# Keys and queries of layer two turned in 32 by 32 blocks by VectorE and moved between partition blocks by ScalarE, in place of transposes on TensorE

## The chip, the cores and the metric

The kernel runs on one core of a Trainium2 chip. The metric is the device time of one execution in microseconds (us). Engines are named as the profile names them: PE is TensorE (PEld its weight loads), DVE is VectorE, ACT is ScalarE, POOL is GpSimd, SP is the engine that issues most DMAs. SBUF is the memory that the engines work on, 128 partitions wide; PSUM is where PE writes its products.

## The reference, cut to what matters

The reference is two layers over 256 tokens of width 2048. The first is a gated linear attention and isn't touched. The second is softmax attention with 16 heads of 128. Keys and queries are projected, normed for each token and head, and multiplied:

```python
proj = h @ w_in.astype(h.dtype)
q = rms_norm(proj[..., :B_INNER].reshape(bsz, t, B_HEADS, B_HEAD_DIM), q_norm_w)
k = rms_norm(proj[..., B_INNER:2 * B_INNER].reshape(bsz, t, B_HEADS, B_HEAD_DIM), k_norm_w)
...
s = jnp.einsum('bchd,bmhd->bhcm', q_n, k_n).astype(jnp.float32) * scale + bias
...
p = jax.nn.softmax(s, axis=-1).astype(v_n.dtype)
return jnp.einsum('bhcm,bmhd->bchd', p, v_n)
```

The norm runs over the head's 128 values of one token, so it is done with tokens on the partitions. The scores contract over these 128 values, so PE needs them on the partitions. Between the two, each head's block of 128 tokens by 128 values has to be transposed.

## The kernel before

All large products are made in chunks. A chunk is 256 rows of a weight matrix by 512 columns: one load of 512 KB from SP's queue into `wt`, one cast on ACT into a rounded part `whi` (line 211), one subtraction on DVE into the remainder `wlo` (line 212), then twelve matmuls on PE in the kind `tokens` (lines 282 to 287, issued at line 259). For each of two row blocks and two token halves these are: activations times `whi`, activations times `wlo`, the activations' own remainder times `whi`. `wt` has four buffers, `whi` and `wlo` have three, so the cast of a chunk can start only when PE has finished the chunk three before it, and the load of a chunk only when the remainder four before it is done. Eight chunks make a block of 512 columns, which is four heads.

`plan` (lines 141 to 166) fixes the order of the chunks: for each of four groups of heads a block of keys, then one of queries, then four blocks of values, then the output projection. Everything else is background work: generators in the lists `bgq` and `bg2`, each cut into steps by `yield`. `block(kind, xb, rate)` calls `tick` after each piece of a chunk, and `tick` runs `rate` steps for each 128 rows, so a block gives 16 steps at rate 1. A scheduler then puts the instructions of each engine into one fixed order, which the engine follows, waiting where an operand isn't there.

For each block of keys or queries the background runs `qk_norm` (lines 1030 to 1063), during the block that follows. ACT squares the block out of PSUM (line 1035), DVE sums by head (1038), POOL makes the reciprocal roots (1040, 1042), DVE multiplies (1047) into a tile `n` with tokens on the partitions. Then PE transposes the eight 128 by 128 pieces against a unit matrix (1057), four into each of two PSUM tiles, and ACT copies each into its place in `dl`: for keys with a scale that holds both norm weights (1062), for queries without (1060). `attend` (1065) follows the queries of a group: score products on PE (1076, 1077), bias and maximum on DVE (1085, 1087), exponentials on ACT (1089), the division on DVE (1095, 1097), the transposition of the weights on PE (1103) and their copy on ACT (1104).

Of the kernel before, what the change touches and what calls it, by code (L numbers as in the profile page):

```python
# [10 lines left out]
AF = mybir.ActivationFunctionType  # L11
# [3 lines left out]
P = 128  # L15
D = 2048
T = 256
# [20 lines left out]
def tile_hybrid_trunk(  # L38
# [12 lines left out]
    act, dve, pool, pe = nc.scalar, nc.vector, nc.gpsimd, nc.tensor  # L51
# [9 lines left out]
    def ps_small():  # L61
        return pss.tile([P, 512], F32, name="pss", tag="pss")

    def wk(tag, bufs=None):

        return work.tile([P, 4, T], F32, name=tag, tag=tag, bufs=bufs)
# [24 lines left out]
    ident = const.tile([P, P], F32, name="ident")  # L91
# [162 lines left out]
    def drain():  # L254
        while now or bgq or bg2:
            step()
# [34 lines left out]
    def chunk(kind, ps, xb, rate=1, pre=None):  # L291
        i = state["use"]
        state["use"] += 1
        while state["next"] < min(i + 1 + LOOK, len(plan)):
            fetch()
        hi, lo = fetched.pop(i)
        kc = KC * 512 // plan[i][3]
        ks = [plan[i][2] * kc + j for j in range(kc)]
        f, ns = KINDS[kind]
        if kind == "half":  # L300
            ps = ps if isinstance(ps, list) else [ps[:, s] for s in range(2)]
            if pre is not None:
                pre(ks[-1])
            for _ in features2(ps, hi, lo, ks, xb):
                tick(rate / 2)
            return
        for j, kt in enumerate(ks):
            if pre is not None:
                pre(kt)
            for s in range(ns):  # L310
                f(ps[:, s], s, j, kt, hi, lo, xb)
                tick(rate / ns)

    def acc(kind):

        shape = {"features": [P, 4, T], "half": [P, 2, 2, T], "tokens": [P, 2, 512]}[kind]
        return psp.tile(shape, F32, name="psp", tag="psp")

    def block(kind, xb, rate=1, pre=None):
        ps = acc(kind)  # L320
        for _ in range(CPH if kind == "half" else CPB):
            chunk(kind, ps, xb, rate, pre)
        return ps
# [33 lines left out]
    def split_tiles():  # L357
        return slot("xb", 32, F32R).rearrange("p (k a t) -> p k a t", k=KT, a=2)
# [34 lines left out]
    xb = split_tiles()  # L393
# [622 lines left out]
    xb = hmem["x"]  # L1016
# [13 lines left out]
    def qk_norm(ps, scale, dst):  # L1030

        ssn = tiny.tile([P, 2, 4], F32, name="ssn", tag="so")
        rn = tiny.tile([P, 2, 4], F32, name="rn", tag="ro")
        sq = wk("cv").rearrange("p h t -> p (h t)")
        act.activation(out=sq, in_=ps.rearrange("p t d -> p (t d)"), func=AF.Square)
        yield 1
        yield 1
        dve.reduce_sum(out=ssn, in_=sq.rearrange("p (t h d) -> p t h d", t=2, d=P), axis=AX.X)  # L1038
        for t in range(2):
            pool.tensor_scalar(out=ssn[:, t, :], in0=ssn[:, t, :], scalar1=1.0 / P, scalar2=bmem["uh"][:, t:t + 1],  # L1040
                               op0=ALU.mult, op1=ALU.add)
        pool.tensor_tensor(out=rn, in0=ssn, in1=nhalf[:, :8].rearrange("p (t h) -> p t h", t=2), op=ALU.pow)  # L1042
        yield 1
        yield 1
        n = wk("cv").rearrange("p h t -> p (h t)").rearrange("p (t d) -> p t d", t=2)
        for t in range(2):
            dve.tensor_tensor(out=n[:, t, :].rearrange("p (h d) -> p h d", d=P),  # L1047
                              in0=ps[:, t, :].rearrange("p (h d) -> p h d", d=P),
                              in1=rn[:, t, :].unsqueeze(2).broadcast_to([P, 4, P]), op=ALU.mult)
        yield 1  # L1050
        yield 1
        for p in range(2):
            pt = ps_small()
            for i in range(2):
                c = (2 * p + i) * P
                for t in range(2):
                    pe.transpose(pt[:, i * T + t * P:i * T + (t + 1) * P], n[:, t, c:c + P], ident)  # L1057
            d = dst[:, 2 * p:2 * p + 2, :].rearrange("p h t -> p (h t)")
            if scale is None:
                act.copy(out=d, in_=pt)  # L1060
            else:
                act.activation(out=d, in_=pt, func=AF.Copy, scale=scale)
            yield 1

    def attend(gi, qn, kn):
# [75 lines left out]

    for gi in range(4):
        c = 1024 * (gi % 2)
        psk = block("tokens", xb)
        if gi == 0:
            drain()
        kn, qn = (hmem["m"][:, b + c:b + c + 1024].rearrange("p (h t) -> p h t", h=4) for b in (8192, 10240))
        bgq.append(qk_norm(psk, bmem["wqk"][:, 0:1], kn))
        psq = block("tokens", xb)
        bgq.append(qk_norm(psq, None, qn))  # L1150
        bgq.append(attend(gi, qn, kn))

# [101 lines left out]
```

## Time and profile before

| What | Value |
|---|---|
| Median of three runs | 1005.47 us (1005.43 to 1006.92) |
| The profiled execution, timed as a whole | 1006.75 us |
| Its span, first to last instruction | 1004.0 us |
| Mean granted clock of PE | 0.999 |
| First and last transposes of keys and queries on PE (line 1057) | 648 and 820 us into the span |
| Idle time of PE over the span, sum of its waits | 2.4 us |

A page of the profile gives for each engine its busy time, its share of the span and its instructions. The chain that ended last is followed back from the last instruction; PE holds 97% of it. In rows of time the columns are start, length, engine, line, operation, what it writes and reads, shapes and count, and in brackets how long the engine stood idle before it and what ended that. In rows of groups they are busy time, mean length of one in ns, idle time before.

### The profile page before, as it was taken

The page shows a single profiled execution, that of the slowest core. Times are in us where ns is not written, and L with a number is a line of the kernel's source. Part 1 is how long each engine was busy: PE and PEld are TensorE (multiplying, and loading weights), DVE is VectorE, ACT ScalarE, POOL GpSimd, SP SyncE. Part 2 cuts the span into 40 slices and gives each one's busy share as a digit, 9 for nine tenths or more (in the row PEclk, how much of TensorE's full clock was granted, in tenths as well). Part 3 has the DMA queues.
Part 4 walks back from the last instruction along what each step waited for, and adds up shares of the span by engine and source line. Part 5 has one row for each costly group of instructions (what it writes and reads, how often), then busy time and mean ns, then how long its engine had stood idle before and what let it go on. Part 6 is the DMA issues. An engine that isn't in the chain of part 4 may idle for free.

```text
span 1004.0 us, 15429 instructions
## 1 busy us (share of the span) xinstructions
PE 997.8 (99%) x5959; PEld 869.5 (87%) x5959; DVE 692.1 (69%) x1129; ACT 528.0 (53%) x791; POOL 61.7 (6%) x78
## 2 busy tenths in 40 slices
PE   9999999999999999999999999999999999999998
PEld 8988888888888899899988888888888888888887
DVE  7789879997998777665767555556565656555554
ACT  8457865564456554544654444446464645444432
POOL 1000001131000000001000000110101010000000
PEclk9999999999999999999999999999999999999999
DMA  9565665555755554545765766665555565555662
GB/s 292 186 185 152 170 187 149 157 157 153 208 166 167 148 148 137 167 137 183 231 193 173 232 207 211 192 184 168 170 166 179 156 188 147 168 169 173 216 216 88
DMA packets 138345, 177.55 MB, mean 177 GB/s; under 512 B 7968, under 2 KB 98464, under 8 KB 138272
## 3 DMA queue, kind: packets, MB, share of 16 engines
q1 hardware_dynamic: 136832, 172.12, 57.8%
q0 software_dynamic: 1152, 4.19, 1.2%
q8 instruction: 46, 0.75, 0.3%
q10 hardware_dynamic: 288, 0.26, 0.1%
q14 instruction: 27, 0.22, 0.1%
HBM read 174.46 MB, written 2.10 MB: 176 GB/s over the span
## 4 chain that ended last, share of the span: by engine, by line
PE 97%; ACT 1%; DMA 1%; DVE 0%; issue 0%; SPq 0%
PE psp L259 86%; PE pss L601 2%; PE pss L259 1%; PE pss L1057 1%; PE pss L1077 1%; PE pss L1133 1%; PE pss L833 1%; DMA g<-in_xT_dram 1%; PE pss L501 1%; PE pss L1103 1%; ACT whi L211 0%; PE pss L856 0%; PE pss L857 0%; PE pss L840 0%; PE pss L858 0%
## 5 line engine op out<-in xcount | busy, mean ns | idle before, releaser
L212 DVE TENSOR_TENSOR wlo<-wt,whi 128x1024 fp32r<-128x1024 f32 (+2 forms) x324 | 391.5, 1212 | 255.5 <-ACT whi L211 251.4
L211 ACT CAST whi<-wt 128x1024 fp32r<-128x1024 f32 (+2 forms) x324 | 336.5, 1039 | 392.3 <-PE psp L259 346.4
L259 PE MATMUL psp<-whi,xb 128*128 128x512 f32 x1024 | 319.5, 392 | 0.0
L259 PE MATMUL psp<-xb,whi 128*128 128x512 f32 (+1 forms) x1088 | 259.4, 380 | 0.3 <-DVE ev L330 0.2
L259 PEld LDWEIGHTS psp<-whi,xb 128*128 128x128 f32 x1024 | 192.0, 188 | 38.9
L259 PEld LDWEIGHTS psp<-xb,whi 128*128 128x128 f32 x1088 | 195.5, 189 | 34.4 <-DVE ev L330 0.6
L259 PE MATMUL psp<-wlo,xb 128*128 128x512 f32 x512 | 200.5, 392 | 0.0
L259 PE MATMUL psp<-xb,wlo 128*128 128x256 f32 x1024 | 148.0, 284 | 0.5 <-DVE wlo L212 0.4
L259 PEld LDWEIGHTS psp<-xb,wlo 128*128 128x128 f32 x1024 | 137.0, 191 | 6.3 <-DVE wlo L212 1.1
L259 PE MATMUL psp<-g,whi 128*128 128x512 f32 (+1 forms) x608 | 132.9, 347 | 0.3 <-DVE ev L330 0.2
L259 PEld LDWEIGHTS psp<-g,whi 128*128 128x128 f32 x608 | 104.7, 190 | 13.3 <-DVE ev L330 0.6
L259 PEld LDWEIGHTS psp<-wlo,xb 128*128 128x128 f32 x512 | 96.2, 188 | 19.6
L259 PE MATMUL psp<-g,wlo 128*128 128x256 f32 x480 | 82.4, 284 | 0.3 <-DVE wlo L212 0.3
L259 PEld LDWEIGHTS psp<-g,wlo 128*128 128x128 f32 x480 | 69.8, 191 | 2.3 <-DVE wlo L212 0.5
L529 DVE SCALAR_TENSOR_TENSOR cv<-raw,sm,cv 128x255 f32<-128x255 f32 (+2 forms) x144 | 63.9, 478 | 3.4 <-ACT cv L527 3.2
L527 ACT ACTIVATE cv<-raw,sm 128x256 f32<-128x256 f32 x48 | 22.4, 509 | 20.6 <-DVE raw L345 20.6
L330 DVE TENSOR_TENSOR ev<-psp,ev 128x512 f32<-128x512 f32 x37 | 25.3, 684 | 0.1
L329 ACT COPY ev<-psp 128x512 f32<-128x512 f32 x37 | 21.4, 577 | 0.0
L1040 POOL TENSOR_SCALAR ssn<-ssn,uh 128x4 f32<-128x4 f32 x16 | 9.2, 590 | 171.7 <-DVE ssn L1038 171.7
L605 DVE TENSOR_TENSOR dl<-pss,dl 128x512 f32<-128x512 f32 (+1 forms) x32 | 16.3, 552 | 2.7 <-PE pss L601 2.7
L1047 DVE TENSOR_TENSOR cv<-psp,rn 128x512 f32<-128x512 f32 x16 | 10.3, 685 | 9.2 <-POOL rn L1042 9.2
L869 POOL TENSOR_TENSOR ro<-so,nhalf 128x8 f32<-128x8 f32 x4 | 6.5, 1635 | 156.0 <-DVE so L867 156.0
(236 smaller groups left out, 742.7 us busy)
## 6 DMA issues: line engine op xcount, KB each, us to landing
wt<-in_b_w_in_dram SPq DMA_DIRECT2D x128, 512.0 KB, 3.7
wt<-in_a_w_in_dram SPq DMA_DIRECT2D x125, 512.0 KB, 4.0
wt<-in_a_w_out_dram SPq DMA_DIRECT2D x32, 512.0 KB, 3.8
wt<-in_b_w_out_dram SPq DMA_DIRECT2D x32, 512.0 KB, 3.4
dl<-in_xT_dram POOLq DMA_DIRECT2D x4, 512.0 KB, 5.6
dl<-in_relb_dram POOLq DMA_DIRECT2D x4, 512.0 KB, 4.7
g<-in_xT_dram SPq DMA_DIRECT2D x7, 256.0 KB, 6.3
out_dram<-ev SPq DMA_DIRECT2D x7, 256.0 KB, 4.1
```

The lines of the kernel that those rows point to most:

```text
L211: cast = act.copy(out=hi[:, js, cs], in_=wt[:, js, cs])
L212: rest = dve.tensor_tensor(out=lo[:, js, cs], in0=wt[:, js, cs], in1=hi[:, js, cs].bitcast(F32), op=ALU.subtract)
L259: state["mm"] = pe.matmul(*args, **kw).ins
L329: act.copy(out=ev, in_=ps[:, :, 1, :])
L330: dve.tensor_tensor(out=ev, in0=ps[:, :, 0, :], in1=ev, op=ALU.add)
L501: pe.matmul(dst, lhsT=lhs, rhs=rbuf[:, gi % 2, 2 * half + part, :], start=(part == 0), stop=(part == 1))
L527: act.activation(out=cv[:, i, :], in_=raw[:, i, :], func=AF.Copy, scale=conv_w(i0 + i, 3))
L529: dve.scalar_tensor_tensor(out=cv[:, i, s:], in0=raw[:, i, :T - s], scalar=conv_w(i0 + i, 3 - s), in1=cv[:, i, s:], op0=ALU.mult, op1=ALU.add)
L601: pe.matmul(dst, lhsT=kq[:, a, i, c:c + P], rhs=rhs, start=(n == 0), stop=(n == 2))
L605: dve.tensor_tensor(out=dl[:, h, :, c], in0=src.rearrange("p (k c) -> p k c", k=2), in1=dec[:, h, c].unsqueeze(1).broadcast_to([P, 2, n]), ...
L833: pe.matmul(ps[:, i * P:(i + 1) * P], lhsT=tt[:, 2 * (h0 + i) + t, :], rhs=vb[:, i, t, :], start=True, stop=True)
L1047: dve.tensor_tensor(out=n[:, t, :].rearrange("p (h d) -> p h d", d=P), in0=ps[:, t, :].rearrange("p (h d) -> p h d", d=P), in1=rn[:, t, :] ...
```

## The change

`qk_norm` no longer uses PE. DVE turns `n` in 32 by 32 blocks into a second tile `u` (two instructions of 128 by 512). Each block is then transposed in itself, but it still stands on the partitions of its tokens. ACT moves the blocks: 16 copies of 32 partitions by 256 elements, each from one of four partition blocks to one of four. For keys one more pass on ACT applies the scale in place, 128 by 1024. The number of steps grows from 8 to 16 for queries and 17 for keys, and the key and query blocks run their background at rate 1.5.

```diff
-        for p in range(2):
-            pt = ps_small()
-            for i in range(2):
-                c = (2 * p + i) * P
-                for t in range(2):
-                    pe.transpose(pt[:, i * T + t * P:i * T + (t + 1) * P], n[:, t, c:c + P], ident)
-            d = dst[:, 2 * p:2 * p + 2, :].rearrange("p h t -> p (h t)")
-            if scale is None:
-                act.copy(out=d, in_=pt)
-            else:
-                act.activation(out=d, in_=pt, func=AF.Copy, scale=scale)
+        u = wk("cv").rearrange("p h t -> p (h t)").rearrange("p (t d) -> p t d", t=2)
+        for t in range(2):
+            dve.transpose(out=u[:, t, :], in_=n[:, t, :])
+            yield 1
+        uv = u.rearrange("p t (h b i) -> p h t b i", b=4, i=32)
+        dv = dst.rearrange("p h (t b i) -> p h t b i", b=4, i=32)
+        for b in range(4):
+            for c in range(4):
+                act.copy(out=dv[32 * c:32 * c + 32, :, :, b, :], in_=uv[32 * b:32 * b + 32, :, :, c, :])
+                if c % 2:
+                    yield 1
+        if scale is not None:
+            d = dst.rearrange("p h t -> p (h t)")
+            act.activation(out=d, in_=d, func=AF.Copy, scale=scale)
             yield 1
...
-        psk = block("tokens", xb)
+        psk = block("tokens", xb, 1.5)
...
-        psq = block("tokens", xb)
+        psq = block("tokens", xb, 1.5)
```

The lines behind the change stand three lower in the new kernel: its copies are at line 1060, the scale at 1065, score products at 1079 and 1080, exponentials at 1092, the copy of the weights at 1107.

The order on ACT at the first keys, from the squares of their block to those of the next, before:

```order
L1035 ACTIVATE cv<-psp 128x1024
L211 CAST whi<-wt 128x1024 x4
L1062 ACTIVATE dl<-pss,wqk 128x512 x2
L211 CAST whi<-wt 128x1024 x4
L1035 ACTIVATE cv<-psp 128x1024
```

And now:

```order
L1035 ACTIVATE cv<-psp 128x1024
L211 CAST whi<-wt 128x1024 x3
L1060 COPY dl<-cv 32x8x32 x14
L211 CAST whi<-wt 128x1024
L1060 COPY dl<-cv 32x8x32 x2
L211 CAST whi<-wt 128x1024
L1065 ACTIVATE dl<-dl,wqk 128x1024
L211 CAST whi<-wt 128x1024 x3
L1035 ACTIVATE cv<-psp 128x1024
```

Fourteen of the sixteen copies now stand together ahead of the fourth cast, where two operations stood behind it. At the same place DVE has, now:

```order
L1038 TENSOR_REDUCE ssn<-cv 128x8
L212 TENSOR_TENSOR wlo<-wt,whi 128x1024
L1047 TENSOR_TENSOR cv<-psp,rn 128x512 x2
L212 TENSOR_TENSOR wlo<-wt,whi 128x1024
L1054 STREAM_TRANSPOSE cv<-cv 128x512 x2
L212 TENSOR_TENSOR wlo<-wt,whi 128x1024 x6
```

The two transpositions stand between two remainders that followed each other before; the first of the fourteen copies waits for the second transposition. PE's order at the end of the first queries, in the chunk whose cast stands behind the fourteen copies, now:

```order
L259 MATMUL psp<-wlo,xb 128x512
L259 MATMUL psp<-whi,xb 128x512 x2
L1079 MATMUL pss<-dl 128x128
L1080 MATMUL pss<-dl 128x256
L1079 MATMUL pss<-dl 128x128
L1080 MATMUL pss<-dl 128x256
L259 MATMUL psp<-wlo,xb 128x512
L259 MATMUL psp<-whi,xb 128x512 x2
```

The second of the first pair opens the chunk; the first scores follow it at once, ahead of the matmul with that chunk's remainder, and they wait for the last copy of the queries. At the second keys ACT also has the exponentials and the copies of the weights. Before:

```order
L211 CAST whi<-wt 128x1024
L1089 ACTIVATE raw,sums<-raw,mx 128x128
L1089 ACTIVATE raw,sums<-raw,mx 128x256
L1089 ACTIVATE raw,sums<-raw,mx 128x128
L1089 ACTIVATE raw,sums<-raw,mx 128x256
L211 CAST whi<-wt 128x1024 x3
L1104 COPY kT<-pss 128x384 x2
L1062 ACTIVATE dl<-pss,wqk 128x512 x2
```

And now:

```order
L211 CAST whi<-wt 128x1024
L1060 COPY dl<-cv 32x8x32 x2
L1092 ACTIVATE raw,sums<-raw,mx 128x128
L1092 ACTIVATE raw,sums<-raw,mx 128x256
L1060 COPY dl<-cv 32x8x32 x3
L211 CAST whi<-wt 128x1024
L1060 COPY dl<-cv 32x8x32 x9
L211 CAST whi<-wt 128x1024
L1060 COPY dl<-cv 32x8x32 x2
L211 CAST whi<-wt 128x1024
L1107 COPY kT<-pss 128x384 x2
L1065 ACTIVATE dl<-dl,wqk 128x1024
```

The fourteen copies are cut by one cast, with one pair of exponentials among them; the third and fourth keys have the same rows. The second and third queries read like the first. At the last queries, which run beside a block of values at rate 1, a cast stands after every four copies.

## The prediction

> **What bounds the kernel now.** I read the page first: engine shares and the chain that ended last. Then the stretches in which layer two makes its keys and queries, the waits there, and last the instructions in order of time around one transposition.
>
> ```profile
> span 1004.0 us, 15429 instructions
> PE 997.8 (99%) x5959; PEld 869.5 (87%) x5959; DVE 692.1 (69%) x1129; ACT 528.0 (53%) x791; POOL 61.7 (6%) x78
> PE 97%; ACT 1%; DMA 1%; DVE 0%; issue 0%; SPq 0%
> ...
> 640.00:660.00 20.00, 20.00 (x94) 16.66 (x93) 10.57 (x10) 8.52 (x9) 3.21 (x3) 1.00 0.63 184
> ...
> 680.00:700.00 20.00, 20.00 (x102) 16.83 (x102) 14.38 (x32) 14.56 (x30) 2.14 (x3) 1.00 0.54 160
> ...
> ACT whi L211 <- PE psp L259: 92.4, 57, 3.0
> ```
>
> TensorE (PE) is busy for the whole of both stretches (window rows: width, then PE, PEld, DVE, ACT, POOL, granted clock, DMA share, GB/s). ScalarE (ACT) has 5 to 11 us free in 20. The wait row, taken over 630 to 840 us, says why that room can't be used at will: 57 casts waited for PE. A cast of weights starts only when PE has let go of its buffer, so the room is cut into pieces between casts that each have a time by which they are needed. In this stretch everything that leaves PE is a gain, and whatever delays a cast or its remainder past that time stops PE.
>
> **What the change removes.** Of the chain over 630 to 830 us, cut to that window:
>
> ```profile
> by line: PE psp L259 90.0%; PE pss L1057 3.5%; PE pss L1077 3.0%; PE pss L1103 2.0%; PE pss L1076 1.6%
> ...
> 648.52 0.87 PE pss L1057 x8
> 649.39 21.78 PE psp L259 x96
> ...
> 677.05 0.22 PE pss L1076 x2
> ...
> 678.36 7.53 PE psp L259 x33
> ...
> 685.89 0.11 PE pss L1103
> ...
> 687.86 9.32 PE psp L259 x41
> ...
> 697.19 0.66 PE pss L1103 x6
> ...
> 819.25 0.87 PE pss L1057 x8
> ...
> L1057 PE MATMUL pss<-ident,cv x64: 270/272/273, 648.4 to 819.9; 128*128 128x128 f32 x64
> ```
>
> 64 transposes go, eight at a time, and eight hold the chain for 0.87 us: 8 x 0.87 = **7.0 us off**. The 272 ns of the last row is the length of one in the pipeline, not its distance from the next (0.87 / 8 = 0.109). The same rows give PE's beat: 96 matmuls in 21.78 us, 0.227 each, so a chunk of twelve lasts 2.72 us.
>
> [...]
>
> **What it adds, and where.** The times around the first keys before, each cast followed by its remainder on VectorE (DVE):
>
> ```profile
> 637.45 1.05 ACT L211 CAST whi<-wt 128x1024 fp32r<-128x1024 f32 x1 [1.67 <-PE psp L259]
> ...
> 642.89 1.05 ACT L211 CAST whi<-wt 128x1024 fp32r<-128x1024 f32 x1 [1.67 <-PE psp L259]
> ...
> 644.40 1.29 DVE L1047 TENSOR_TENSOR cv<-psp,rn 128x512 f32<-128x512 f32 x2 [1.93 <-POOL rn L1042]
> ...
> 645.61 1.06 ACT L211 CAST whi<-wt 128x1024 fp32r<-128x1024 f32 x1 [1.67 <-PE psp L259]
> 645.61 2.35 DVE L212 TENSOR_TENSOR wlo<-wt,whi 128x1024 fp32r<-128x1024 f32 x2
> ...
> 647.90 0.62 PE L259 MATMUL psp<-whi,xb 128*128 128x512 f32 x2
> ...
> 648.33 1.05 ACT L211 CAST whi<-wt 128x1024 fp32r<-128x1024 f32 x1 [1.66 <-PE psp L259]
> ...
> 649.40 1.23 DVE L212 TENSOR_TENSOR wlo<-wt,whi 128x1024 fp32r<-128x1024 f32 x1 [1.44 <-ACT whi L211]
> ```
>
> Call the casts at 637.45, 642.89, 645.61 and 648.33 A, C, D and E. E waited for the chunk whose last matmul is the first of the pair at 647.90; the second of the pair, at 648.13, opens the next chunk. Three buffers mean that E's chunk comes two chunks later: at 648.13 + 2 x 2.72 = 653.57 once the transposes are gone. Its second matmul needs E's remainder at **653.80**. Before, that remainder is done at 650.63, over 3 us early.
>
> The new operations have these nearest rows:
>
> ```profile
> L654 DVE STREAM_TRANSPOSE g<-g 128x1024 f32<-128x1024 f32 x1 | 2.1, 2127 | 0.2 <-ACT g L570 0.2
> ...
> L657 DVE STREAM_TRANSPOSE nbrT<-nbr x1: 216/216/216, 248.7 to 248.7; 128x32 f32<-128x32 f32 x1
> ...
> L570 ACT COPY g<-dl 32x256 f32<-32x256 f32 x4 | 1.6, 402 | 0.0
> ...
> 243.82 1.64 ACT L570 COPY g<-dl 32x256 f32<-32x256 f32 x4
> ...
> 217.91 0.91 ACT L527 ACTIVATE cv<-raw,sm 128x256 f32<-128x256 f32 x2 [0.92 <-DVE raw L345]
> ...
> L1060 ACT COPY dl<-pss 128x512 f32<-128x512 f32 x8 | 4.3, 586 | 0.0
> ...
> 671.93 1.07 ACT L1060 COPY dl<-pss 128x512 f32<-128x512 f32 x2
> ```
>
> A transposition of 128x512 lies between 1.06 (half of 2127) and 1.14 us (on the line through both rows); I take 1.07, two are 2.15. A copy of 32 partitions by 256 in runs of 32 is exactly the four-copy row: 1.64 / 4 = **0.41 us**, with no overlap. Lower bound: the two 586 ns copies end in 1.07, so they overlap by 0.10, which would make 0.31. Upper bound: the pair of 256-element operations on all partitions, 0.91 / 2 = 0.455. Copies from one partition block to another stand in no row; I take 0.41, the row of the same shape.
>
> **The ladder at the first keys.** By the order, DVE does the norm products (to 645.69), C's remainder (about 1.15, half of the 2.35: to 646.8), the two transpositions (to **648.95**), then D's remainder (to 650.2; its chunk needs it at 651.08, so that is free). ACT does D, then fourteen copies that wait for the transpositions: 648.95 + 14 x 0.41 = 654.7. Only then comes E: to 655.75, its remainder to 657.0. PE wanted it at 653.80: **3.2 us of standing still**. Then two copies, the next cast, the scaling pass and the cast after: 656.6, 657.7, 658.7, 659.8, remainder 661.0. That chunk needs it at 659.24 + 3.2 = 662.4, so the queue has caught up. What was ACT's room (1.66 us before each cast) is spent in one piece, ahead of one cast.
>
> **First, second and third queries.** Same ladder, no scaling. Here PE's order puts four score products (677.05 to 678.36: 1.31 us) between E's first matmul and the one that needs the remainder, and they need the last two copies: 655.75 + 0.82 = 656.6, scores to 657.9. Without a stall they would end at 653.80 + 1.31 = 655.1: **2.8 us** each.
>
> **Second to fourth keys.** Attention stands in the same stretch:
>
> ```profile
> 679.69 1.28 ACT L1089 ACT_TABLE_LOAD   x1
> ...
> 689.78 0.40 ACT L1089 ACTIVATE raw<-raw,mx 128x128 f32<-128x128 f32 x1
> ...
> 691.60 1.05 ACT L211 CAST whi<-wt 128x1024 fp32r<-128x1024 f32 x1
> ```
>
> From A's start the transpositions end 11.5 us later at the first keys; here a pair of score reductions replaces C's remainder ahead of them, so about 11.4 again. Then ACT has fourteen copies (5.74), one pair of exponentials (half of 689.78 to 691.60, 0.91), casts D and E (2.1) and E's remainder (1.25): 21.4 us after A. PE needs it 653.80 - 637.45 = 16.35 later, plus its attention work in between (685.89 to 687.86 and 0.66: 2.63), which is 18.98. **2.4 to 2.6 us**; I take 2.5. For the second keys the exponentials' table load (1.28) holds A back by about 1.2 more: 3.7.
>
> **Last queries.** A cast stands after every four copies: 1.05 + 4 x 0.41 = 2.69 in a chunk of 2.72. E starts at 648.95 + 1.64 = 650.6, its remainder is done at 652.9: free.
>
> **Sum.** Stalls 3.2 + 3 x 2.8 + 3.7 + 2 x 2.5 = 20.3; less 7.0: **+13.3 us**. The profiled execution took 1006.75 around its span of 1004.0, so it would take 1020; the median of the three timed runs, 1005.47, lies 1.3 lower: **1019**. The higher rate of 1.5 only moves steps earlier; at 24 turns a block the two norms and the attention (some 39 steps in 48) are still done in time. Bounds: at 0.31 a copy each of seven places loses 1.4 less, 1009; at 0.455 it loses 0.63 more, 1023.
>
> **The rivals.** *The copies overlap after all*, as the full-width ones do: 1009, or 1007.5 to 1012 if only in part. For it: the L1060 pair. Against it: the four-copy row.
>
> *A transpose holds PE for its whole 0.272 us*: 64 of them would be 17.4 off instead of 7.0, 1008.6 in all. The chain row is against it. [...]
>
> *The copies fit* (the other side). The place is the gap from 648.95 to 653.80, into which fourteen copies, a cast and a remainder must go. At 0.20 us a copy no place stalls, and the time is 1005.47 - 7.0 = 998.5; the change pays below about 0.27 (13.3 / 7 / 14 = 0.14 under 0.41). No row of 256 elements is that short.
>
> *More comes late after the stall.* Two mechanisms:
>
> ```profile
> wt<-in_b_w_in_dram SPq DMA_DIRECT2D x69, 512.0 KB, 3.7
> ...
> 1000.00:1004.00 4.00, 0.49 (x5) 0.29 (x3) 0.85 (x2) 0.00 (x0) 0.00 (x0) 0.86 0.19 66
> ```
>
> The remainder at 657.0 also frees the raw buffer for the load four chunks on, queued on SP behind it: 657.0 + 3.7 = 660.7, wanted at 659.2 + 3.2 = 662.4. Covered by 1.7 us; a load slower by 1 us more than that would cost 7 us in all. And where PE idles, its granted clock falls: 0.86 over the last four microseconds. Four microseconds at 0.86 after each stall are 0.65 us, 4.6 in seven places: 1024; with late loads too, up to 1032. [...]
>
> **Chances.** Forecast (1012 to 1024.5): 0.62. Overlap: 0.13, and a transpose of 0.272 us 0.01. More comes late (1024.5 to 1033): 0.12. Copies fit: 0.07. A balance within 0.2%, which is about what a measurement of this kernel can tell from no change (1003.5 to 1007.5): 0.05. The range 1007 to 1030 takes in the copy's bounds and most of the late case. Faster 0.07, same 0.05, slower 0.88.
>
> **What would show it.** No L1057 on PE; 128 L1060 copies of 0.40 us; seven PE waits of 2 to 4 us for ACT's casts or DVE's remainders, none at the last queries; PE's busy time down by at most 7 us. It is wrong if the copies follow each other in under 0.3 us, if PE waits at the scores longer than at the remainders, or if the waits sit elsewhere.

## The result, and the profile after

| | Before | After |
|---|---|---|
| Median (lowest to highest) | 1006.11 us (1005.43 to 1006.92) | 1016.39 us (1015.21 to 1016.9) |
| Span of the profiled execution | 1004.0 us | 1014.9 us |

The ratio is 1.0099, with a 95% interval of 1.0087 to 1.0112: slower by 10.3 us, in the direction forecast and 2.6 us short of the forecast's 1019. The page of the new kernel:

```profile
span 1014.9 us, 15425 instructions
...
PE 997.3 (98%) x5895; PEld 863.9 (85%) x5895; DVE 700.4 (69%) x1145; ACT 575.0 (57%) x907; POOL 64.8 (6%) x78
...
PE 84%; ACT 6%; DVE 4%; issue 2%; POOL 2%; DMA 1%; SPq 0%; DVEq 0%; POOLq 0%
```

PE has 64 instructions fewer, and its share of the chain that ended last fell from 97% to 84%: the chain now runs over other engines in places where it ran on PE alone (the share says where the chain runs, not how much was lost). ACT has 47 us more, 116 instructions more. The waits of PE over 630 to 850 us say where (engine and line, what it waited for, us in total, times, the longest):

```profile
PE psp L259 <- ACT whi L211: 6.2, 7, 1.3
PE psp L259 <- DVE wlo L212: 3.3, 5, 0.8
PE pss L1079 <- ACT dl L1060: 1.0, 3, 0.3
```

Before, PE waited for nothing in this stretch. Now it waits for casts, for their remainders, and for the queries that the scores read (line 1079). ACT and DVE at the first keys, with PE's matmuls around the stall, in order of time (start, length, engine, operation, and in brackets the idle time before and what ended it):

```profile
645.82 1.05 ACT L211 CAST whi<-wt 128x1024 fp32r<-128x1024 f32 x1 [1.67 <-PE psp L259]
...
646.97 1.30 DVE L1054 STREAM_TRANSPOSE cv<-cv 128x512 f32<-128x512 f32 x2
...
648.30 5.80 ACT L1060 COPY dl<-cv 32x256 f32<-32x256 f32 x14 [1.42 <-DVE cv L1054]
...
653.56 0.39 PE L259 MATMUL psp<-whi,xb 128*128 128x512 f32 x1
654.13 1.04 ACT L211 CAST whi<-wt 128x1024 fp32r<-128x1024 f32 x1
...
655.21 1.23 DVE L212 TENSOR_TENSOR wlo<-wt,whi 128x1024 fp32r<-128x1024 f32 x1 [5.83 <-ACT whi L211]
...
655.23 0.50 PE L259 MATMUL psp<-whi,xb 128*128 128x512 f32 x1 [1.28 <-ACT whi L211]
...
656.49 0.69 PE L259 MATMUL psp<-wlo,xb 128*128 128x512 f32 x1 [0.76 <-DVE wlo L212]
...
656.97 1.06 PE L259 MATMUL psp<-whi,xb 128*128 128x512 f32 x2
...
656.99 1.14 ACT L1065 ACTIVATE dl<-dl,wqk 128x1024 f32<-128x1024 f32 x1
```

This is the ladder of the forecast, rung by rung: two transpositions, fourteen copies behind each other, cast E at 654.13, its remainder at 655.21, the matmul that needs it at 656.49. The matmul at 653.56 is the last of the chunk ahead of E's, the one at 655.23 is E's first. By start times the stall is read without modelled ends: 653.56, 655.23 and 656.49 where the beat is 0.227, so (1.67 - 0.23) + (1.26 - 0.23) = 2.47 us. The last pair of matmuls, 1.06 us where a pair took 0.62, shows a second cost: PE runs at half speed for a while. More of that below. The other kinds of places, PE alone, first queries, second keys and third keys:

```profile
681.05 0.50 PE L259 MATMUL psp<-whi,xb 128*128 128x512 f32 x1 [1.16 <-ACT whi L211]
681.89 0.49 PE L1079 MATMUL pss<-dl 128*128 128x128 f32 x2 [0.34 <-ACT dl L1060]
...
705.50 0.50 PE L259 MATMUL psp<-wlo,xb 128*128 128x512 f32 x1 [0.28 <-DVE wlo L212]
...
709.05 0.49 PE L259 MATMUL psp<-whi,xb 128*128 128x512 f32 x1 [0.77 <-ACT whi L211]
710.31 0.50 PE L259 MATMUL psp<-wlo,xb 128*128 128x512 f32 x1 [0.77 <-DVE wlo L212]
...
761.94 0.50 PE L259 MATMUL psp<-whi,xb 128*128 128x512 f32 x1 [0.31 <-ACT whi L211]
763.20 0.50 PE L259 MATMUL psp<-wlo,xb 128*128 128x512 f32 x1 [0.76 <-DVE wlo L212]
```

A bracket leaves out what the last matmul's modelled row is longer than its beat: 0.39 - 0.23 = 0.16, or 0.50 - 0.23 = 0.27 where the last matmul had itself waited. With that, the first queries lost 1.16 + 0.16 + 0.34 + 0.27 = 1.93, the second keys 0.28 + 0.16 + 0.77 + 0.16 + 0.77 + 0.27 = 2.41, the third keys 0.31 + 0.16 + 0.76 + 0.27 = 1.50. The second and third queries read like the first, the fourth keys like the third, and the last queries have no wait. In all 2.47 + 3 x 1.93 + 2.41 + 2 x 1.50 = **13.7 us of stalls**.

**The clock.** Stretches of the new kernel (limits in us, width, busy time and instructions of PE, PEld, DVE, ACT, POOL, granted clock, DMA share, GB/s), cut into pieces of 3.41 us, the length of one fall of the clock, so laid that the changes of the clock fall on their limits:

```profile
653.22:656.63 3.41, 1.37 (x6) 0.59 (x5) 1.23 (x1) 3.30 (x7) 0.00 (x0) 1.00 0.00 0
656.63:660.04 3.41, 3.41 (x9) 2.67 (x10) 2.17 (x2) 2.44 (x3) 0.00 (x0) 0.50 0.55 164
...
707.83:711.24 3.41, 1.88 (x8) 1.02 (x7) 1.52 (x2) 3.33 (x7) 0.00 (x0) 1.00 0.25 93
711.24:714.66 3.42, 3.42 (x10) 2.64 (x9) 1.91 (x2) 2.42 (x5) 0.00 (x0) 0.50 0.79 208
731.72:735.14 3.42, 2.26 (x11) 1.54 (x9) 0.23 (x1) 3.31 (x8) 0.00 (x0) 1.00 0.14 55
```

For 3.41 us after the first and the second keys' stalls the clock is 0.50, which by the clock costs half of that, 1.7 us each, **3.4 us**. The five other stalls, such as that of the second queries in the last row, cost none. Together 13.7 + 3.4 - 7.0 = 10.1 us, of the 10.9 by which the spans differ. Of the rest 0.2 comes from ahead of this stretch (the squares of the first keys start at 638.62 us, before at 638.40), and 0.6 is not accounted for.

### The profile page after: what moved, and what is told of

The parts are those of the page before. It is cut to its first block, busy times and chain, and to the rows that moved or that the text cites. A ratio compares the mean times of both kernels' runs of the same rounds, so it can differ in the third digit from the quotient of the medians.

```text
span 1014.9 us, 15425 instructions
## 1 busy us (share of the span) xinstructions
PE 997.3 (98%) x5895; PEld 863.9 (85%) x5895; DVE 700.4 (69%) x1145; ACT 575.0 (57%) x907; POOL 64.8 (6%) x78
## 4 chain that ended last, share of the span: by engine, by line
PE 84%; ACT 6%; DVE 4%; issue 2%; POOL 2%; DMA 1%; SPq 0%; DVEq 0%; POOLq 0%
PE psp L259 74%; ACT dl L1060 3%; ACT whi L211 2%; PE pss L601 2%; DVE wlo L212 2%; POOL rn L1042 1%; POOL ssn L1040 1%; DVE ssn L1038 1%; PE pss L259 1%; PE pss L1136 1%; DVE cv L1047 1%; PE pss L833 1%; ACT raw L1092 1%; DMA g<-in_xT_dram 1%; DVE cv L1054 1%
## 5 line engine op out<-in xcount | busy, mean ns | idle before, releaser
L259 PE MATMUL psp<-whi,xb 128*128 128x512 f32 x1024 | 324.4, 395 | 6.2 <-ACT whi L211 6.2
L259 PEld LDWEIGHTS psp<-g,whi 128*128 128x128 f32 x608 | 104.7, 190 | 13.3 <-DVE ev L330 0.6
L1060 ACT COPY dl<-cv 32x256 f32<-32x256 f32 x128 | 51.7, 404 | 14.3 <-DVE cv L1054 6.6
L1040 POOL TENSOR_SCALAR ssn<-ssn,uh 128x4 f32<-128x4 f32 x16 | 12.2, 777 | 179.4 <-DVE ssn L1038 179.4
L1047 DVE TENSOR_TENSOR cv<-psp,rn 128x512 f32<-128x512 f32 x16 | 10.3, 686 | 12.0 <-POOL rn L1042 12.0
```

Source lines behind the costliest of these rows:

```text
L259: state["mm"] = pe.matmul(*args, **kw).ins
L1060: act.copy(out=dv[32 * c:32 * c + 32, :, :, b, :], in_=uv[32 * b:32 * b + 32, :, :, c, :])
```

## The experiments

Two stories could explain the loss. Mine: the copies stand as a block on ACT's queue ahead of a cast with a due time, and the delay follows from their number, their price and the transpositions' price ahead of them. The rivals: the higher rate of the background by itself, or the work added to ACT and DVE, wherever it stands.

**Only the rate.** The kernel before, with the key and query blocks at rate 1.5:

```diff
-        psk = block("tokens", xb)
+        psk = block("tokens", xb, 1.5)
...
-        psq = block("tokens", xb)
+        psq = block("tokens", xb, 1.5)
```

> The kernel before with nothing changed but the rate of 1.5 in the key and query blocks; the transposes stay on TensorE. Theory (the loss is TensorE standing still behind ScalarE's copies): no change, 1005 to 1007 us, no waits of TensorE in the stretch from 640 to 820 us, L1057 still 64 times. Rival (the denser background, not the copies, takes the time): 1010 us or more, with waits of TensorE beside the attention's work.

1005.96 against 1005.91 us, ratio 1.0002 (0.9993 to 1.0011), and no wait of PE from 630 to 850 us. The rate has no part in the loss.

**Without the transposition.** The kernel before; ACT copies the untransposed pieces from SBUF in the same two passes, so PE's transposes are left out, nothing is put in their place, and the scores are made from blocks that aren't transposed:

```diff
-            pt = ps_small()
+            pt = n.rearrange("p t (h d) -> p h t d", d=P)[:, 2 * p:2 * p + 2]
...
-                    pe.transpose(pt[:, i * T + t * P:i * T + (t + 1) * P], n[:, t, c:c + P], ident)
+                    pass
-            d = dst[:, 2 * p:2 * p + 2, :].rearrange("p h t -> p (h t)")
+            d = dst[:, 2 * p:2 * p + 2, :].rearrange("p h (t d) -> p h t d", d=P)
```

> The kernel before without its 64 transposes of keys and queries: ScalarE copies the untransposed tile in their place, with the same 16 operations, so that the part left out is the transposition itself. Theory (the transposes hold TensorE for 0.109 us each): 7.0 us less than before, 999 us, no new waits. Rival 1 (each holds it for 0.272 us): 17 us less, 989 us. Rival 2 (what leaves TensorE there is hidden anyway): 1006 us.

998.76 against 1005.91 us, ratio 0.9929 (0.9914 to 0.9945): 7.15 us for 64 transposes, 0.11 each, which bears out the 7.0 read from the chain. As PE bounds this kernel as before (its waits sum to 3.1 us of a span of 997.3), that is about what there is to win by turning keys and queries off PE.

**The same work in another order.** The kernel after, with every four copies kept by the scheduler (`issue_after`) behind the cast of the chunk fetched last, and more steps between them so that each group meets another chunk:

```diff
-            for c in range(4):
-                act.copy(out=dv[32 * c:32 * c + 32, :, :, b, :], in_=uv[32 * b:32 * b + 32, :, :, c, :])
-                if c % 2:
-                    yield 1
+            with tc.issue_after(splits[state["next"] - 1][0]):
+                for c in range(4):
+                    act.copy(out=dv[32 * c:32 * c + 32, :, :, b, :], in_=uv[32 * b:32 * b + 32, :, :, c, :])
+            yield 1
+            yield 1
+            yield 1
+            yield 1
...
-        psk = block("tokens", xb, 1.5)
+        psk = block("tokens", xb, 2)
...
-        psq = block("tokens", xb, 1.5)
+        psq = block("tokens", xb, 2)
```

> The changed kernel with the same instructions, only that each four copies are put behind the youngest cast of weights, so that a cast stands after every four copies (steps per norm 26 and 27 at rate 2 instead of 16 and 17 at 1.5). Theory (it is the place of the copies ahead of a cast, not their amount): the waits at the first to third queries and first keys vanish; at the second to fourth keys, where the exponentials share the stretch, up to 1 us each may be left; 999 to 1002 us, faster than both. Rival (the amount of ScalarE's work, or VectorE's transpositions ahead of a remainder, is what costs): 1012 us or more.

1000.27 against 1005.91 us, ratio 0.9944 (0.9931 to 0.9956). The page's engines:

```profile
PE 991.7 (99%) x5895; PEld 862.2 (86%) x5895; DVE 700.0 (70%) x1145; ACT 573.2 (57%) x907; POOL 64.3 (6%) x78
```

ACT has the same 907 instructions and is as busy (573.2 against 575.0 us), DVE too. ACT in order of time at the first keys:

```profile
648.38 1.66 ACT L1061 COPY dl<-cv 32x256 f32<-32x256 f32 x4 [1.42 <-DVE cv L1054]
650.06 1.05 ACT L211 CAST whi<-wt 128x1024 fp32r<-128x1024 f32 x1
651.14 1.66 ACT L1061 COPY dl<-cv 32x256 f32<-32x256 f32 x4
652.82 1.05 ACT L211 CAST whi<-wt 128x1024 fp32r<-128x1024 f32 x1
```

The cast that started at 654.13 starts at 650.06, and PE's waits over 640 to 860 us shrink to one row:

```profile
PE psp L259 <- DVE wlo L212: 0.7, 2, 0.3
```

So 16 us lie between two orders of the same instructions, and the rival that counts added work wherever it stands falls. This order stays 1.6 us behind the next kernel. About 1.0 of it are these two waits, at the third and fourth keys (0.34 us each, and 0.16 that a bracket leaves out); the rest was not followed up.

**The same block on another engine.** The kernel after, with all 128 copies on POOL, and then with every second one there:

```diff
-                act.copy(out=dv[32 * c:32 * c + 32, :, :, b, :], in_=uv[32 * b:32 * b + 32, :, :, c, :])
+                pool.tensor_copy(out=dv[32 * c:32 * c + 32, :, :, b, :], in_=uv[32 * b:32 * b + 32, :, :, c, :])
```

```diff
-                act.copy(out=dv[32 * c:32 * c + 32, :, :, b, :], in_=uv[32 * b:32 * b + 32, :, :, c, :])
+                (pool.tensor_copy if c % 2 else act.copy)(out=dv[32 * c:32 * c + 32, :, :, b, :], in_=uv[32 * b:32 * b + 32, :, :, c, :])
```

> The changed kernel with the 128 copies between partition blocks on GpSimd instead of ScalarE; VectorE's transpositions, the scale and the rate stay. Theory: ScalarE's casts are as early as before, 999 to 1002 us, unless GpSimd's copies take so long that the score products wait for them (L685 shows 1.04 us for 1024 elements on 32 partitions, so 0.3 to 0.4 us each, 5 to 6.5 us for sixteen, which would still be in time). Rival (the loss lies in VectorE's transpositions or in the rate): 1012 us or more. VectorE's remainders may be longer while GpSimd copies (one of 1.49 instead of 1.23 us stands at 298 us of the trace before, beside GpSimd's copies).

> The changed kernel with every second copy on GpSimd, so that 7 instead of 14 copies stand ahead of the cast at the first keys and at the queries. Theory (a place costs nothing until copies, cast and remainder together pass the time at which TensorE wants them): at the first keys 648.3 + 7 x 0.41 + 1.05 + 1.25 = 653.4 us against a need at 653.8, so no stall; at the second to fourth keys at most 0.5 us; 998.5 to 1001 us. Rival (each copy on ScalarE costs its share): half of the loss of 17 us, about 1008 us.

All on POOL: 998.63 against 1005.91 us, ratio 0.9929 (0.9916 to 0.9943). Half there: 998.50 against 1005.80, ratio 0.9926 (0.9909 to 0.9943). Both beat the kernel before and the kernel after, and reach the 998.76 of the kernel that leaves the transposition out: the whole 7 us are kept. With all on POOL, in order of time at the first keys, of POOL and of ACT:

```profile
647.83 11.83 POOL L1060 COPY dl<-cv 32x256 f32<-32x256 f32 x16 [3.73 <-DVE cv L1054]
...
648.04 1.05 ACT L211 CAST whi<-wt 128x1024 fp32r<-128x1024 f32 x1 [1.67 <-PE psp L259]
...
650.76 1.05 ACT L211 CAST whi<-wt 128x1024 fp32r<-128x1024 f32 x1 [1.67 <-PE psp L259]
```

The block of sixteen is now 11.83 us long, where 5 to 6.5 had been expected and fourteen took 5.80 on ACT, and costs nothing, since no cast stands behind it: the casts follow PE's beat of 2.72 again. With half on each:

```profile
647.74 2.89 ACT L1060 COPY dl<-cv 32x256 f32<-32x256 f32 x7 [1.42 <-DVE cv L1054]
...
647.84 4.28 POOL L1060 COPY dl<-cv 32x256 f32<-32x256 f32 x8 [3.80 <-DVE cv L1054]
...
650.66 1.05 ACT L211 CAST whi<-wt 128x1024 fp32r<-128x1024 f32 x1
```

Seven copies still stand ahead of the cast and delay it, but 2.89 us fit into ACT's slack and PE waits nowhere from 630 to 850 us. So the cost doesn't go with the number of copies: below the slack it is nothing. Seven copies of 0.41 are as long as fourteen of 0.207, and the rival "the copies fit" had set the point without stalls at 0.20, with a time of 998.5. The time came, but the 0.20 is a slip: in the forecast's own gap, 4.85 us from 648.95 to 653.80, a cast of 1.06 and a remainder of 1.25 leave 2.54 us, 0.18 a copy. With the transpositions 0.85 us shorter, as measured, it is 0.24.

**A dearer transposition.** The ladder came out shorter than forecast, and its first rung is the one that measured differently. The kernel after, in its own order, with DVE reading and writing the 128x512 piece with strides; the blocks then stand in wrong places, so attention works on misplaced values:

```diff
-            dve.transpose(out=u[:, t, :], in_=n[:, t, :])
+            dve.transpose(out=u[:, t, :].rearrange("p (a c) -> p a c", c=32), in_=n[:, t, :].rearrange("p (c a) -> p a c", a=16))
```

> The changed kernel with the same order on every engine, only that VectorE's 16 transpositions read and write with strides (so the values land elsewhere and the attention is computed from wrongly placed ones). Rows L654 and L668 of before are strided and took 2.1 us for 1024 elements, the changed kernel's contiguous ones 0.69 us for 512. Theory (the forecast's price of 1.07 us was that of a strided transposition, and each microsecond that the copies start later is one more of TensorE's standing still): transpositions of about 1.06 us, 0.75 us more stall in each of seven places, 1016.4 + 5.2 = 1021.6 us at the same granted clock; with half-speed stretches of 3.4 us behind more than two of the seven stalls, 1.7 us more for each, up to 1030 us. Rival (the shape, not the strides, sets the price): 0.69 us each and 1016.4 us.

1023.97 against 1005.80 us, ratio 1.018 (1.0165 to 1.0195); 7.6 us over the kernel after. The group of the transpositions (ns least, median, most) in the kernel after, and in this one:

```profile
L1054 DVE STREAM_TRANSPOSE cv<-cv x16: 666/696/708, 647.0 to 829.9; 128x512 f32<-128x512 f32 x16
```

```profile
L1054 DVE STREAM_TRANSPOSE cv<-cv x16: 1011/1050/1057, 646.7 to 837.4; 128x512 f32<-128x512 f32 x16
```

The same operation on the same number of elements takes 0.70 us in one piece and 1.05 with strides. Two of them now end 0.70 us later, and at the first keys PE's wait for cast E grows from 1.28 to 1.97. At the first keys, the first queries and the third keys:

```profile
655.63 0.50 PE L259 MATMUL psp<-whi,xb 128*128 128x512 f32 x1 [1.97 <-ACT whi L211]
...
683.36 0.50 PE L259 MATMUL psp<-whi,xb 128*128 128x512 f32 x1 [1.85 <-ACT whi L211]
...
766.28 0.50 PE L259 MATMUL psp<-whi,xb 128*128 128x512 f32 x1 [0.77 <-ACT whi L211]
```

The rows of PE's waits over 630 to 850 us:

```profile
PE psp L259 <- ACT whi L211: 9.8, 7, 2.0
PE psp L259 <- DVE wlo L212: 3.6, 5, 0.8
PE pss L1079 <- ACT dl L1060: 1.0, 3, 0.3
```

The waits for casts grew by 3.6 us and the others by 0.3, 3.9 in all, where 5.2 had been expected: each stall grew by 0.69 at the first keys and the three queries, but by only 0.3 at the second keys and 0.46 at the third and fourth. Why the places with attention take less of the delay was not followed up. Most of the rest is the clock. Stretches of this kernel, cut in the same way:

```profile
652.65:656.06 3.41, 1.44 (x6) 0.69 (x4) 0.45 (x1) 3.30 (x8) 0.00 (x0) 1.00 0.05 19
656.06:659.47 3.41, 2.65 (x7) 2.10 (x7) 2.00 (x2) 3.39 (x4) 0.00 (x0) 0.50 0.41 91
659.47:662.89 3.42, 3.42 (x9) 2.65 (x9) 1.23 (x1) 0.91 (x2) 0.00 (x0) 0.50 0.83 229
679.95:683.37 3.42, 1.57 (x8) 0.95 (x7) 0.03 (x1) 3.31 (x8) 0.00 (x0) 1.00 0.24 93
...
714.09:717.50 3.41, 3.41 (x10) 2.64 (x9) 1.90 (x2) 2.54 (x4) 0.00 (x0) 0.50 0.76 195
...
765.29:768.70 3.41, 1.88 (x7) 1.18 (x7) 1.76 (x2) 3.35 (x6) 0.00 (x0) 1.00 0.22 70
768.70:772.11 3.41, 3.41 (x10) 2.63 (x9) 1.90 (x2) 2.61 (x4) 0.00 (x0) 0.50 0.77 203
```

PE was busy for 2.65 + 3.42 + 3.41 + 3.41 = 12.9 us at half speed, which costs 6.4, where the kernel after lost 3.4. So 3.9 + 3.0 = 6.9 of the 7.3 us between the two spans are accounted for.

## Why the prediction was right, and where its sizes were off

| Term | Forecast, us | Measured, us |
|---|---|---|
| 64 transposes off PE | -7.0 | -7.15 (its own experiment) |
| Stall at the first keys | 3.2 | 2.5 |
| First, second, third queries, each | 2.8 | 1.9 |
| Second keys | 3.7 | 2.4 |
| Third and fourth keys, each | 2.5 | 1.5 |
| Last queries | 0 | 0 |
| Sum of the stalls | 20.3 | 13.7 |
| Clock after the stalls | 0 | 3.4 |
| Net | +13.3 | about +10.0 by these terms; medians +10.3, spans +10.9 |

- **The mechanism held.** Seven places stall, in the waits named, and the last queries don't. PE waits 1.0 us at the scores and 3.3 for remainders, and its busy time fell by 0.5 us, both within the signs named. The stalls themselves were named too long: 2 to 4 us each, and five of the seven are under 2. It is the place of the copies ahead of a due cast that costs, and not the added work as such, as the reordered kernel shows.
- **The copy's price held.** Fourteen take 5.80 us, 0.414 each, against 0.41. The rival in which they overlap is dead; of the three rows the four-copy row of the same shape was the one to trust.
- **The transposition was mis-sized.** The step that put a transposition of 128x512 between 1.06 and 1.14 us failed: two ended after 1.30 us, not 2.15. By the ladder that takes 0.85 off each of seven stalls, 6.0 of the 6.6 us between 20.3 and 13.7. My row was of another layout, and I had bounded the price only by size. The strided kernel, with 2.00 us for two, shows the layout as the cause of the difference in price and moves the stall at the first keys by the 0.70 us that the ladder says: to 3.17, where 2.15 had given 3.2. It bears out this share for the first keys and the queries only. At the second to fourth keys (1.3, 1.0 and 1.0 under the forecast) 0.70 us of delay moved the stalls by 0.3 to 0.46, so there it may explain less than 0.85: with its forecast price nearly put back these stalls are 2.7, 2.0 and 2.0 us, not 3.7, 2.5 and 2.5. A further term of the ladder beside attention was too large, and no run isolates it. The table load was charged with 1.2 at the second keys, which lost 0.9 more than the third.
- **The clock was put among the rivals and came in part.** "More comes late" priced it at 0.65 us after each of seven stalls; it was 1.7 after two of them. The matmul inside the stall at the first keys didn't keep half speed away: the row 653.22:656.63 holds E's first matmul and has PE busy for 1.37 of 3.41 us, and the clock of the next row is 0.50. The other half of this rival, loads that come late, showed in no wait of PE or of ACT's casts.
- **Two errors hid each other.** With the transposition's true price and no clock the sum would have been 7.3 us, 1013; with the forecast's price and the clock's 3.4 to 6.4 us, 1022 to 1025, and the strided kernel's 1023.97 lies there. That the forecast came within 2.6 us is in part luck.

## What to carry to other kernels

Before work goes to a half-idle engine, list what else stands in its queue with a time by which it is needed: free time in pieces does not hold a block of work longer than a piece, and here the order of the same instructions was worth 16 us, more than twice the gain sought. Then either put the work behind the urgent instructions, cut it below the slack (seven copies cost nothing, fourteen 13.7 us of stalls), or give it to an engine on which nothing is due, even if it is slower there (sixteen copies in 11.83 us on POOL, fourteen in 5.80 on ACT, and 998.63 us). And a row of the same operation gives a price only if its layout is the same too (128x512 took 0.70 us in one piece and 1.05 with strides).

## What the runs showed of the hardware beyond that

- **Half speed came in stretches of 3.41 us.** The clock fell to 0.50 at 656.63 and 711.24 us in the kernel after, and at 656.06, 714.09 and 768.70 in the strided one. Four of the five falls lasted 3.41 us, and the one at 656.06 lasted 6.83. The distances from fall to fall are 54.61, 58.03 and 54.61 us, within 0.1 us of 16, 17 and 16 times 3.41. PE wasn't idle throughout ahead of a fall: in the 3.41 us before, it was busy for 1.37 and 1.88 us in the kernel after, and for 1.44 and 1.88 before the first and the third fall of the strided one. Nor does its busy time alone say which stall is followed by half speed: the clock stayed at 1.00 behind the stretch with 2.26 us busy in the kernel after, but in the strided one also behind a stretch with 1.57 (with score products in it), where it fell behind one with 1.88. What decides it is not shown; no run isolates it.
- **Some copies on POOL were long, and two of these ran beside remainders on DVE.** The group of the copies with all of them on POOL (ns least, median, most):

```profile
L1060 POOL COPY dl<-cv x128: 386/395/1485, 647.8 to 821.2; 32x256 f32<-32x256 f32 x128
```

Half take under 0.4 us, about as on ACT (0.40), but the mean is 0.64 (82.3 us for 128) and the longest is nearly four times the least. The first, at 647.83, took 1.29 us beside a remainder on DVE that had started at 647.69 and took 1.18; another, at 651.96, took 1.38 beside one of 1.23 from 651.85. They ended 0.25 and 0.26 us after the remainders. Whether the remainders made them long is not shown: no run takes DVE's work away.
